# A hybrid attention and state-space layer on one core: values as plain fp32 in column halves, a strip for the S5 kernel matrix, x loaded first

## The chip, the cores and the metric

The kernel runs on one core of a Trainium2 chip. Five engines work side by side and meet through semaphores: TensorE (PE in the profile, with its weight loads as PEld), VectorE (DVE), ScalarE (ACT), GpSimd (POOL) and SyncE (SP), whose queue issues every DMA of this kernel in program order. The metric is the device time of one execution in microseconds (us), as a median over runs.

## The reference, cut to what matters

One decoder layer over 512 positions of width 1024, all in fp32:

```python
h = rmsnorm(x, norm1_g) * (1 + sc1) + sh1            # sc1, sh1 from silu(c) @ w_ada + b_ada
zq, zkc, zvc, zks, zvs, zkw, zvw, zg, zs = split(h @ w_in)
# attention: 8 query heads, 2 key/value heads, width 64, causal
#   three branches per head: compressed blocks, selected blocks, window
o_b = softmax(q k_b^T / 8, mask_b) @ v_b;   o = sum over b of gate_b * o_b
# state space: 32 groups of 16 channels, one 64-wide complex diagonal state per group
x_t = a * x_(t-1) + B u_t;   y_t = Re(C x_t) + d * u_t     # then gelu and glu
x = x + gt1 * (concat(rmsnorm(o), rmsnorm(y)) @ w_o)
h = rmsnorm(x, norm2_g) * (1 + sc2) + sh2
x = x + gt2 * ((silu(a) * b) @ w_down),  a, b = causal_conv3(h @ w_up)
return rmsnorm(x, normf_g)
```

With 512 positions all 8 blocks of 64 keys are selected and the window covers everything, so "selected" and "window" are two causal attentions with their own keys and values.

## The kernel before, in words

The work is written as named tasks, and the string `ORDER` lists them. A scheduler takes them in that order and sets each engine's own instruction stream; every engine then runs its stream strictly in order. A table `PICK` names, for single operations, the engine or the buffer pool that differs from the default. Buffers come from rings, and a load waits until the ring's next slot is free: `raw` has 4 slots of 512 KB, `unit` (weights split in two) has 4, `pt` has 4.

Most products are made of three fp32r matmuls (`mm3`, lines 120 to 123): both operands are split into a high and a low part, by a copy on ACT and a subtraction on DVE or POOL (`split`, line 109). Some products are single fp32 matmuls, each of which stands in the trace as two matmul instructions.

1. Start. Tasks `x`, `xn`: load the four 128-row tiles of x, normalise, transpose (`xT`, L458). Tasks `a`, `p`: 512 KB weight pieces for scale and shift, multiplied by silu(c) on PE (L385), turned to columns (L394). Tasks `step`, `pw`, `ri`: the powers of the state's decay, on small tiles named `gpt`, mostly on POOL (L200), and their transposes `ri` (L317). Task `bct`: transposes of B and C (`bt<-raws`, L336). Task `ws`: the state-space columns of `w_in`. Task `z`: 8 steps, each scaling one 128-row slab of xT into h (`hh`, `hl`) and making 12 matmuls of 512 columns into the four `zs` banks.
2. `W`: matrices of powers times B, made on POOL (L348, L349) and transposed on PE; `U`: u re-laid; `L`: the states within chunks of 8 positions; `chain`: the scan over the 64 chunks; `zk`, `zv`, `zq`: the other columns of `w_in`; `hid`, `comp`: the compressed keys and values.
3. Attention, 16 units (4 query tiles `qt`, 2 groups `g`, 2 pairs of heads `hp`). `S`: scores (L832), mask and maximum on DVE (L846), exponentials on ACT. `O`: for each of the qt+1 key tiles four transposes (L882) of the weights into one PSUM bank, a split of it into `pt` (L109), and four matmuls of 256 columns (L892). There the values `VT` stand as [high | low], 64 + 64 columns, so the result has the high part's product in PSUM rows 0 to 63 and the low part's in rows 64 to 127; both heads lie side by side in the columns. After each unit the low half is copied out (`tl`) and added to the high half (`oT`, L906). There are 40 key-tile steps in the 16 units.
4. State-space output, placed between the attention units: `K` makes the kernel matrices K(0) to K(7) of each group; `M` holds them as a block triangle, 8 x 8 blocks of 16 x 16 per group; `Y` multiplies u by M and the chunk states by `VV` in fp32, with the two halves of the groups in the two column halves of PE (`ps[hf * 64:(hf + 1) * 64, ...]`, L1004). M is cleared on POOL (L954); for every 4 groups, K's rows are copied out in eight small pieces `kt` (L990 and L67), d on the diagonal is added there, and eight DMAs, one per block row r, write (r+1) blocks each.
5. `gl`, `R`, `F`, `N`: glu, output projection, residual, second norm. Then up (`up`, `eup`), convolution, and down (`dn`).

## Time and profile before

| | |
|---|---|
| median of 3 runs | 789.72 us (788.53 to 789.72) |
| profiled execution, own time | 788.76 us |
| its span, first to last instruction | 787.0 us |
| busy: PE, DVE, ACT, POOL | 715.0, 503.1, 308.9, 310.7 us |
| mean granted TensorE clock | 0.949 of full speed |

The profile gives, per engine, which instructions ran, how long, and what ended the idle time before them. "L109" is line 109 of the kernel; a helper's line is shared by all that call it, so the tile names tell the tasks apart. Busy times of matmuls are modelled and overlap, so the distance between two starts says more than a matmul's own duration. The granted clock is given as a share of full speed.

### The profile page before, as it was taken

What the parts mean: (1) busy time and instruction counts of PE and PEld (TensorE: products, weight loads), DVE (VectorE), ACT (ScalarE), POOL (GpSimd) and SP (SyncE); (2) the same over time, 40 slices, a digit from 0 to 9 for tenths busy, and PEclk for the clock granted to TensorE, in tenths of its full rate; (3) what the DMA queues carried; (4) which work ended last, traced back from release to release, by engine and by line L of the source; (5) the groups of instructions that cost most, each with busy time, mean ns of one, the idle gap of its engine ahead of it and who ended that gap; (6) DMA issues with size and microseconds to landing.
All of it is one profiled execution on the core that took longest, in us unless ns stands there. A gap on an engine that the chain in (4) does not pass through costs nothing.

```text
span 787.0 us, 11037 instructions
## 1 busy us (share of the span) xinstructions
PE 715.0 (91%) x3947; PEld 582.9 (74%) x3947; DVE 503.1 (64%) x1135; ACT 308.9 (39%) x648; POOL 310.7 (39%) x318
## 2 busy tenths in 40 slices
...
GB/s 301 316 243 121 81 142 174 328 184 2 20 13 29 4 19 253 51 1 1 6 198 123 53 161 104 114 131 134 106 131 85 107 105 111 107 83 105 53 1 107
DMA packets 30458, 86.69 MB, mean 110 GB/s; under 512 B 8296, under 2 KB 8740, under 8 KB 30373
## 3 DMA queue, kind: packets, MB, share of 16 engines
...
HBM read 82.71 MB, written 2.10 MB: 108 GB/s over the span
## 4 chain that ended last, share of the span: by engine, by line
PE 66%; DVE 17%; POOL 7%; ACT 4%; issue 4%; DMA 1%; SPq 0%; POOLq 0%; DVEq 0%; ACTq 0%
PE up L123 9%; PE up L121 9%; PE up L122 9%; PE dn L122 5%; PE dn L123 5%; PE dn L121 5%; DVE Ss L846 2%; PE pv L892 1%; PE eup L123 1%; PE eup L122 1%; PE eup L121 1%; PE y L1004 1%; POOL gpt L200 1%; PE sc L832 1%; PE zs L121 1%
## 5 line engine op out<-in xcount | busy, mean ns | idle before, releaser
L121 PE MATMUL up<-h2h,uup 128*128 128x512 f32 x320 | 126.5, 395 | 0.0
L122 PE MATMUL up<-h2l,uup 128*128 128x512 f32 x320 | 126.3, 395 | 0.0
L123 PE MATMUL up<-h2h,uup 128*128 128x512 f32 x320 | 126.2, 394 | 0.0
L1167 DVE SCALAR_TENSOR_TENSOR us<-up,cst,us 128x511 f32<-128x511 f32 x80 | 59.8, 747 | 63.0 <-ACT us L1165 61.9
L1165 ACT ACTIVATE us<-up,cst 128x512 f32<-128x512 f32 x40 | 31.1, 778 | 107.3 <-PE up L123 107.2
L123 PEld LDWEIGHTS up<-h2h,uup 128*128 128x128 f32 x320 | 60.1, 188 | 14.1
L122 PEld LDWEIGHTS up<-h2l,uup 128*128 128x128 f32 x320 | 60.0, 188 | 14.1
L121 PEld LDWEIGHTS up<-h2h,uup 128*128 128x128 f32 x320 | 60.1, 188 | 14.0
L122 PE MATMUL dn<-udn,ghs 128*128 128x512 f32 x176 | 68.5, 389 | 0.0
L123 PE MATMUL dn<-udn,ghs 128*128 128x512 f32 x176 | 68.5, 389 | 0.0
L121 PE MATMUL dn<-udn,ghs 128*128 128x512 f32 x176 | 68.0, 389 | 0.0
L109 DVE TENSOR_TENSOR uup<-rup,uup 128x1024 fp32r<-128x1024 f32 x32 | 40.9, 1280 | 13.3 <-ACT uup L64 13.1
L73 POOL TENSOR_SCALAR Ss<-Ss,sm 128x384 f32<-128x384 f32 (+3 forms) x40 | 25.1, 641 | 47.3 <-DVE sm L855 34.2
L71 POOL CAST uup<-rup 128x1024 fp32r<-128x1024 f32 x6 | 7.1, 1186 | 82.6 <-PE up L123 80.4
L121 PEld LDWEIGHTS dn<-udn,ghs 128*128 128x128 f32 x176 | 33.0, 188 | 6.9
L122 PEld LDWEIGHTS dn<-udn,ghs 128*128 128x128 f32 x176 | 33.0, 188 | 6.9
L123 PEld LDWEIGHTS dn<-udn,ghs 128*128 128x128 f32 x176 | 33.0, 188 | 6.8
L832 PE MATMUL sc<-KS,QS 128*128 128x288 f32 (+2 forms) x128 | 33.2, 373 | 5.2 <-DVE mx L846 2.2
L892 PE MATMUL pv<-pt,VT 128*128 128x256 f32 x160 | 33.3, 314 | 3.0 <-DVE pt L109 1.3
L851 ACT ACTIVATE Ss<-Ss,mx 128x128 f32<-128x128 f32 (+3 forms) x64 | 35.0, 550 | 0.0
L109 DVE TENSOR_TENSOR udn<-rdn,udn 128x1024 fp32r<-128x1024 f32 x17 | 22.4, 1316 | 19.0 <-ACT udn L64 11.2
L64 ACT ACTIVATE uup<-rup 128x1024 fp32r<-128x1024 f32 x28 | 29.4, 1049 | 9.4 <-PE up L123 8.1
...
## 6 DMA issues: line engine op xcount, KB each, us to landing
rup<-in_w_up_dram SPq DMA_DIRECT2D x44, 512.0 KB, 3.3
rdn<-in_w_down_dram SPq DMA_DIRECT2D x22, 512.0 KB, 3.2
mid<-in_w_ada_dram SPq DMA_DIRECT2D x16, 512.0 KB, 4.0
adap<-in_w_ada_dram SPq DMA_DIRECT2D x8, 512.0 KB, 7.5
adaa<-in_w_ada_dram SPq DMA_DIRECT2D x8, 512.0 KB, 8.5
adag<-in_w_ada_dram SPq DMA_DIRECT2D x8, 512.0 KB
adab<-in_w_ada_dram SPq DMA_DIRECT2D x7, 512.0 KB, 3.6
xt<-in_x_dram SPq DMA_DIRECT2D x4, 512.0 KB, 5.5
```

The costliest lines, as they stand in the source:

```text
L64: A.activation(dst, src, AF.Copy, **({} if s is None else {"scale": s}))
L73: P.tensor_scalar(dst, src, s, 1.0, op0=ALU.mult, op1=ALU.mult)
L109: eng.tensor_tensor(out=lo, in0=src, in1=f(hi), op=ALU.subtract)
L121: PE.matmul(ps, w[0], m[0], start=start, stop=False)
L122: PE.matmul(ps, w[0], m[1], start=False, stop=False)
L123: PE.matmul(ps, w[1], m[0], start=False, stop=stop)
L832: PE.matmul(ps[:, :n], v.QS[:, h, qs], v.KS[:, g, x, c0:c0 + n], start=x == 0, stop=x == 1)
L846: V.tensor_tensor_reduce(out=dst, in0=src, in1=msk, scale=1.0, scalar=init, op0=ALU.add, op1=ALU.max, accum_out=ao)
L851: A.activation(Sv[:, br, :nk], Sv[:, br, :nk], AF.Exp, bias=mx[:, e, 1 + br:2 + br], scale=0.125, accum_out=sm[:, e, 1 + br:2 + br])
L892: PE.matmul(po[:, :256], VT[:, kc, br, g], pT[:, x, br * 256:(br + 1) * 256], start=kc == 0 and br == 0 and x == 0, stop=kc == qt > 0 and ...
L1165: A.activation(u_, ps, AF.Identity, bias=cv[:, 3, c_:c_ + 1], scale=cv[:, 2, c_:c_ + 1])
L1167: V.scalar_tensor_tensor(u_[:, d:], ps[:, :S - d], cv[:, 2 - d, c_:c_ + 1], u_[:, d:], op0=ALU.mult, op1=ALU.add)
```

## The change

Seven things.

- Order of the start: x is loaded first and normalised before anything else; the loads of a, p and ws follow in the order in which the z steps use them, and z steps stand between them in `ORDER`. The pieces of a and p, which before were spread over `raw` and `pt`, are nearly all in `raw` now. h's low part `hl` (8 subtractions of 128x512) is made on DVE and no longer on POOL; squares of x are summed on ACT and no longer on DVE; x is scaled on ACT and DVE, no longer on POOL.
- Attention, `O`: `VT`, `VC` and the transposed weights stay fp32 and whole. A key-tile step copies the PSUM bank once (14 of the 40 copies on DVE, 26 on ACT), and makes four fp32 matmuls of 64 x 128 columns; head e of the pair writes PSUM rows 64e to 64e+63. The four units of a query tile share one bank, which is copied out once (`oT`).
- `K` and `M`: d enters as four more small matmuls per 4 groups (`dg`), K's bank is copied whole into a strip with 112 zeros ahead of it (`kz`), and one DMA per group and half writes 64 partitions of 512 bytes, each reading the strip 16 elements further on. M is not cleared any more.
- `W`: four steps of 8 groups and two halves of 4 powers, channel ahead of power in the layout, power 0 taken as 1 from the table `RI`; the four small copies on POOL go. 24 operations of 512 elements instead of 24 of 448.
- `zu`: u is laid out with the position innermost, to match W.
- The three operations of one of the eight `VV` steps go from DVE to POOL; five subtractions of the up weights go from DVE to POOL, two of the down weights too.
- `ORDER` differs in many places behind the start as well.

```diff
@@ ORDER, first lines @@
-x3 ident c rows x0 x1 x2 sp bc step vt silu p1 dT pw ri a1 bct0 xn0 xn1 bct1 a0 p0 xn2 ws1 Bb1 ws3 xn3 ws0 z0 z1 z2 z3 a2 p2 a3 ws2 p3 z4 z5
+ident c x0 xn0 x1 xn1 x2 xn2 x3 xn3 rows sp vt silu a0 p0 ws0 step a1 p1 z0 z1 ws1 z2 dT a2 p2 z3 ws2 pw bc a3 p3 z4 z5 ws3 ri bct0 bct1 z6
...
-        v.Z2 = v.zu[:, 0].rearrange("p (g r c) -> p g r c", r=4, c=C)
+        v.Z2 = v.zu[:, 0].rearrange("p (g c r) -> p g c r", r=4, c=C)
...
-        v.scv = p2.tile([128, 2, 2, 4, T, C], F32, tag="x", name="scv")
-
-    @per("W", *range(8))
-    def _(gq):
+        v.scv = p2.tile([128, 2, 8, 2, C, 4], F32, tag="x", name="scv")
+        P.memset(RI[:, 0, 0], 1.0)
+        P.memset(RI[:, 0, 1], 0.0)
+
+    @per("W", 0, 1, 2, 3)
+    def _(q):
         v.nw = getattr(v, "nw", 0) + 1
-        wb, wt = v.scv[:, v.nw % 2, 0], v.scv[:, v.nw % 2, 1]
-        we = kn(f"e_W{gq}", "P", "V")
-        cpy(kn(f"e_Wc{gq}", "P", "A", "V"), wb[:, :, 0], Bb1[:, gq * 4:gq * 4 + 4])
-        powers(wb[:, :, 1:], Bb1, Bb2, gq * 4, 4, 1, T - 1, wt[:, :, 1:], EN[we])
-        ps = psum(f"W{gq}", f"W{gq}", "ms", "tr")
-        for g in range(4):
-            PE.transpose(ps[:, g * 128:(g + 1) * 128], wb[:, g].rearrange("p t c -> p (t c)"), ident)
-        cpy(kn(f"e_We{gq}", "A", "V"), v.W[:, gq * 4:gq * 4 + 4], ps.rearrange("p (g n) -> p g n", g=4))
+        wb = v.scv[:, v.nw % 2]
+        for h in range(2):
+            tmp = sw(f"wt{q}{h}").rearrange("p (g c t) -> p g t c", g=8, c=C)
+            powers(wb[:, :, h].rearrange("p g c t -> p g t c"), Bb1, Bb2, q * 8, 8, 4 * h, 4, tmp, EN[kn(f"e_W{q}{h}", "P", "V")])
+        for hf in range(2):
+            ps = psum(f"W{q}{hf}", f"W{q}{hf}", "ms", "tr")
+            for g in range(4):
+                PE.transpose(ps[:, g * 128:(g + 1) * 128], wb[:, hf * 4 + g].rearrange("p h c t -> p (h c t)"), ident)
+            cpy(kn(f"e_We{q}{hf}", "A", "V"), v.W[:, q * 8 + hf * 4:q * 8 + hf * 4 + 4], ps.rearrange("p (g n) -> p g n", g=4))
...
-    VT = p1.tile([128, NT, 2, 2, 128], F32R, tag="vt", name="VT")
+    VT = p1.tile([128, NT, 2, 2, 64], F32, tag="vt", name="VT")
...
-        split(VT[:, t, :, :, 0:64], VT[:, t, :, :, 64:128], src, V)
+        cpy(kn(f"e_VT{t}", "A", "V"), VT[:, t], src)
...
+    def half_pt(n, name):
+
+        if v.pT is None:
+            v.pT = pt([128, 2, 512], F32, name)
+            return v.pT[:, 0, :n]
+        p, v.pT = v.pT[:, 1, :n], None
+        return p
...
-        po = psum("pv", f"pv{un}", "pv")
-        pc_ = psum(f"pc{un}", f"pc{un}", "tr", "pv", "ms")
+        if qt not in v.po:
+            v.po[qt] = psum(f"po{qt}", f"po{qt}", "pv", "ms", "acc")
+        c = slice(u * 128, (u + 1) * 128)
+
+        def half(e):
+            return v.po[qt][e * 64:(e + 1) * 64, c]
+        pc_ = psum(f"pc{un}", f"pc{un}", "tr", "ms", "acc")
         PE.transpose(pc_[:, :128], scz[ui], ident)
-        pz = pt([128, 2, 128], F32R, f"pz{un}")
-        split(pz[:, 0], pz[:, 1], pc_[:, :128], V)
+        pz = (p2.tile([128, 256], F32, tag="ada", name=f"pz{un}", bufs=kn("b_ada", 2, 1, 3, 4)) if kn(f"pz{un}", "ada", "sw") == "ada" else sw(f"pz{un}"))[:, :128]
+        cpy(kn(f"e_pz{un}", "A", "V"), pz, pc_[:, :128])
         for kc in range(qt + 1):
-            pc_ = psum(f"p{un}{kc}", f"p{un}{kc}", "tr", "ms")
+            pc_ = psum(f"p{un}{kc}", f"p{un}{kc}", "tr", "ms", "acc")
             for br in range(2):
                 for e in range(2):
                     o = (br * 2 + e) * 128
                     PE.transpose(pc_[:, o:o + 128], v.Ss[:, ui, e, br, kc * 128:(kc + 1) * 128], ident)
-            pT = pt([128, 2, 512], F32R, f"pt{un}{kc}")
-            if kn(f"e_pt{un}{kc}", "V", "P") == "P":
-                ps_ = sw(f"ps{un}{kc}")
-                cpy(kn(f"e_ps{un}{kc}", "A", "V"), ps_, pc_)
-                split(pT[:, 0], pT[:, 1], ps_, P, kn(f"h_ps{un}{kc}", "A", "P"))
-            else:
-                split(pT[:, 0], pT[:, 1], pc_, V)
+            pT = half_pt(512, f"pt{un}{kc}")
+            cpy(kn(f"e_pT{un}{kc}", "AV"[kc % 2], "VA"[kc % 2]), pT, pc_)
             for br in range(2):
-                for x in range(2):
-                    PE.matmul(po[:, :256], VT[:, kc, br, g], pT[:, x, br * 256:(br + 1) * 256],
-                              start=kc == 0 and br == 0 and x == 0, stop=kc == qt > 0 and br == 1 and x == 1)
+                for e in range(2):
+                    o = (br * 2 + e) * 128
+                    PE.matmul(half(e), VT[:, kc, br, g], pT[:, o:o + 128], start=kc == 0 and br == 0, stop=kc == qt > 0 and br == 1)
             if kc == 0:
                 for e in range(2):
-                    for x in range(2):
-                        PE.matmul(po[:, e * 128:(e + 1) * 128], VC[:, g, e], pz[:, x], start=False,
-                                  stop=qt == 0 and e == 1 and x == 1)
-        tl = (p2.tile([128, 256], F32, tag="ada", name=f"tl{un}", bufs=kn("b_ada", 2, 1, 3, 4)) if kn(f"tl{un}", "ada", "sw") == "ada" else sw(f"tl{un}"))[:64, :256]
-        cpy(kn(f"e_tl{un}", "A", "V"), tl, po[64:128, :256])
-        eo, hi_ = V, po[0:64, :256]
-        if kn(f"e_oT{un}", "V", "P") == "P":
-            eo, hi_ = P, sw(f"th{un}")[:64, :256]
-            cpy(kn(f"e_th{un}", "A", "V"), hi_, po[0:64, :256])
-        for e in range(2):
-            eo.tensor_tensor(out=oT[e * 64:(e + 1) * 64, 2 * g + hp], in0=hi_[:, e * 128:(e + 1) * 128],
-                             in1=tl[:, e * 128:(e + 1) * 128], op=ALU.add)
+                    PE.matmul(half(e), VC[:, g, e], pz, start=False, stop=qt == 0)
+        v.no[qt] = v.no.get(qt, 0) + 1
+        if v.no[qt] == 4:
+            v.oT[qt] = p1.tile([128, 4, 128], F32, tag="oT", name=f"oT{qt}", bufs=kn("b_oT", 3, 4, 2))
+            cpy(kn(f"e_oT{qt}", "A", "V"), v.oT[qt].rearrange("p c n -> p (c n)"), v.po[qt])
...
     @task("M")
         v.M = p2.tile([128, G, T, C], F32, tag="h0", name="M")
-        P.memset(v.M, 0.0)
...
-        for n, (o, w) in enumerate(((0, C), (C, 112))):
+        for n, o, w in ((1, C, 112), (0, 0, C)):
             for g in range(4):
                 g_ = gq * 4 + g
                 m = v.VV[:, g_, 0:T - 1].rearrange("p t c -> p (t c)") if n else C1[:, g_]
-                PE.matmul(ps[32 * g:32 * g + 32, o:o + w], Bb1[:, g_:g_ + 2].rearrange("p g c -> p (g c)"), m, start=True, stop=True,
+                PE.matmul(ps[32 * g:32 * g + 32, o:o + w], Bb1[:, g_:g_ + 2].rearrange("p g c -> p (g c)"), m, start=True, stop=n == 1,
                           tile_position=(0, 32 * g))
-        kt = p1.tile([16, 4, T, C], F32, tag="sw", name=f"kt{gq}", bufs=kn("b_sw", 3, 4, 5))
+        dg = p1.tile([16, 4, C], F32, tag="dg", name=f"dg{gq}", bufs=2)
+        EN[kn(f"e_dg{gq}", "V", "P")].tensor_tensor(out=dg, in0=bc(ident[:16, 0:1], (0, 4), (1, C)), in1=bc(dT[:, gq * 4:gq * 4 + 1], (1, 4), (0, C)), op=ALU.mult)
         for g in range(4):
-            row = ps[32 * g:32 * g + C]
-            V.scalar_tensor_tensor(kt[:, g, 0], ident[:C, 0:C], dT[:, gq * 4 + g:gq * 4 + g + 1], row[:, 0:C], op0=ALU.mult, op1=ALU.add)
-            cpy("AV"[g % 2], kt[:, g, 1:].rearrange("p t c -> p (t c)"), row[:, C:128])
-        for r in range(T):
-            nc.sync.dma_start(v.M[r * C:(r + 1) * C, gs, T - 1 - r:], kt[:, :, 0:r + 1])
+            PE.matmul(ps[32 * g:32 * g + 32, 0:C], ident[0:C, 0:32], dg[:, g], start=False, stop=True, tile_position=(0, 32 * g))
+
+        if gq % 2 == 0 or v.kz is None:
+            v.kz = sw(f"kz{gq}")[:, :480].rearrange("p (a n) -> p a n", a=2)
+            EN[kn(f"e_kz{gq}", "P", "V")].memset(v.kz[:, :, 0:112], 0.0)
+            v.nk = 0
+        kz = v.kz[:, v.nk]
+        v.nk += 1
+        if v.nk == 2:
+            v.kz = None
+        cpy(kn(f"e_kt{gq}", "A", "V"), kz[:, 112:240], ps[:, :128])
+        for g in range(4):
+            for hf in range(2):
+                o = kz[32 * g:32 * g + C, hf * 64:hf * 64 + 1]
+                nc.sync.dma_start(v.M[hf * 64:hf * 64 + 64, gq * 4 + g].rearrange("p t c -> p (t c)"), bc(o, (C, 4), (1, 128)))
```

SP's stream at the start, before; `adap` and `adaa` are pieces of p and a, `rins` of ws, `raws` holds B and C:

```order
L168 DMA xt<-in_x_dram 128x1024 x3
L204 DMA sp<-in_ssm_dram 32x145
L208 DMA raws<-in_bc_dram 32x4096
L370 DMA adap_150<-in_w_ada_dram 128x1024
L370 DMA adap_152<-in_w_ada_dram 128x1024
L370 DMA adaa_222<-in_w_ada_dram 128x1024
L370 DMA adaa_224<-in_w_ada_dram 128x1024
L370 DMA adaa_319<-in_w_ada_dram 128x1024
L370 DMA adaa_321<-in_w_ada_dram 128x1024
L115 DMA rins_374<-in_w_in_dram 128x1024
```

And the same place now:

```order
L168 DMA xt<-in_x_dram 128x1024 x4
L164 DMA rows<-in_vec_dram 108x128
L204 DMA sp<-in_ssm_dram 32x145
L370 DMA adaa_201<-in_w_ada_dram 128x1024
L370 DMA adaa_203<-in_w_ada_dram 128x1024
L370 DMA adap_220<-in_w_ada_dram 128x1024
L370 DMA adap_222<-in_w_ada_dram 128x1024
L208 DMA raws<-in_bc_dram 32x4096
L596 DMA cst<-in_cst_dram 128x768
L370 DMA adac_769<-in_w_ada_dram 128x1024
L115 DMA rins_238<-in_w_in_dram 128x1024
L370 DMA adaa_263<-in_w_ada_dram 128x1024
```

The first ws piece stands behind one a and one p now, and the four `raw` slots are full when it comes.

PE's stream at the start, before, from the first a and p products on:

```order
L385 MATMUL mp_154<-adap_150,cs 32x256 x4
L385 MATMUL mp_154<-adap_152,cs 32x256 x4
L385 MATMUL ma_226<-adaa_222,cs 32x256 x4
L458 MATMUL xT_268<-ident,xt 128x128 x4
L394 MATMUL mp_154<-ones,rowp_155 128x1 x2
L385 MATMUL ma_226<-adaa_224,cs 32x256 x4
L458 MATMUL xT_274<-ident,xt 128x128 x4
L317 MATMUL ri<-ident,gpt 128x32
L336 MATMUL bt_241<-ident,raws 128x32 x16
```

And now, from the last transposes of x to the first z product; a further `ri`, the second `bt` and a1's columns stand between these two pieces:

```order
L458 MATMUL xT_181<-ident,xt 128x128 x4
L317 MATMUL ri<-ident,gpt 128x32
L336 MATMUL bt_538<-ident,raws 128x32 x16
L254 MATMUL vt<-ident,rows 128x108
L385 MATMUL ma_205<-adaa_201,cs 32x256 x4
L385 MATMUL ma_205<-adaa_203,cs 32x256 x4
L385 MATMUL mp_224<-adap_220,cs 32x256 x4
L385 MATMUL mp_224<-adap_222,cs 32x256 x4
```

```order
L385 MATMUL ma_267<-adaa_263,cs 32x256 x4
L385 MATMUL ma_267<-adaa_265,cs 32x256 x4
L385 MATMUL mp_286<-adap_282,cs 32x256 x4
L394 MATMUL ma_267<-ones,rowa_268 128x1 x2
L121 MATMUL zs_300<-uins_240,hh 128x512
```

All transposes of x now precede the a and p products, and the first a product stands behind `ri` and `bt`.

DVE's stream in the third query tile's units, before: each `pt` row is the second half of a split, the copy on ACT being the first:

```order
L846 ISA Ss,mp_3472<-sc_3479,cst,mp_3472 128x256
L846 ISA mp_3472 128x1
L109 TENSOR_TENSOR pt_3155<-p_3150,pt_3155 128x512
L846 ISA Ss,mp_3472<-sc_3479,cst,mp_3472 128x256
L846 ISA mp_3472 128x1
L846 ISA Ss,mx_3470<-sc_3484,cst,mp_3472 128x128
L846 ISA mx_3470 128x1
L109 TENSOR_TENSOR pt_3167<-p_3162,pt_3167 128x512
```

And now, in another unit of that query tile, where `pt` on DVE is a copy and stands alone:

```order
L67 COPY pt_2950<-p_2945 128x512
L848 ISA Ss,mx_3046<-sc_3055,cst,mp_3048 128x256
L848 ISA mx_3046 128x1
L848 ISA Ss,mx_3046<-sc_3071,cst,mp_3064 128x256
L848 ISA mx_3046 128x1
L848 ISA Ss,mx_3046<-sc_3055,cst,mp_3048 128x256
L848 ISA mx_3046 128x1
L67 COPY pt_2950<-p_2956 128x512
```

One `pt` buffer now takes two steps' weights, where before it took the high and the low part of one.

## Rows read from the trace of the kernel before

**Rows 1.** Busy by stage: length, PE, PEld, DVE, ACT, POOL, clock, DMA share, GB/s.

```profile
0.00:43.70 43.70, 25.60 (x200) 16.20 (x200) 21.15 (x55) 22.47 (x43) 31.22 (x61) 1.00 0.88 312
43.70:72.00 28.30, 27.59 (x136) 25.83 (x133) 20.81 (x24) 7.64 (x13) 28.14 (x31) 0.94 0.52 171
72.00:120.00 48.00, 48.00 (x338) 40.59 (x337) 24.90 (x42) 21.33 (x45) 35.41 (x38) 1.00 0.38 116
120.00:185.00 65.00, 53.42 (x388) 36.91 (x386) 43.72 (x59) 11.83 (x26) 51.07 (x55) 0.87 0.60 202
185.00:240.00 55.00, 40.23 (x282) 31.39 (x283) 48.56 (x238) 33.24 (x121) 23.14 (x19) 0.77 0.08 14
240.00:400.00 160.00, 145.52 (x924) 121.43 (x924) 134.76 (x457) 98.25 (x250) 77.08 (x76) 0.94 0.16 53
400.00:770.00 370.00, 369.60 (x1669) 306.78 (x1669) 198.00 (x245) 108.55 (x141) 60.09 (x36) 0.99 0.31 104
```

**Rows 2.** PE in order of time, 0 to 100 us: start, length, instruction.

```profile
14.57 2.27 PE L385 MATMUL mp<-adap,cs 128*32 128x256 f32 x16 [3.14 <-DMA adap<-in_w_ada_dram]
...
21.87 0.31 PE L317 MATMUL ri<-ident,gpt 32*128 32x32 f32 x1
22.00 1.93 PE L336 MATMUL bt<-ident,raws 32*128 32x32 f32 x16
...
43.69 0.63 PE L121 MATMUL zs<-uins,hh 128*128 128x512 f32 x1
...
71.81 0.39 PE L123 MATMUL zs<-uins,hl 128*128 128x512 f32 x1
72.03 1.04 PE L544 MATMUL W<-ident,scv 128*128 128x128 f32 x8
```

**Rows 3.** DMA issues by line: size, median us from issue to landing.

```profile
rup<-in_w_up_dram SPq DMA_DIRECT2D x44, 512.0 KB, 3.3
```

**Rows 4.** POOL in order of time, around 20 us.

```profile
20.21 0.58 POOL L200 TENSOR_TENSOR gpt<-gpt,sp 32x64 f32<-32x64 f32 x2
```

**Rows 5.** POOL, groups by form, 30 to 180 us: count, busy us, mean ns.

```profile
L348 POOL TENSOR_TENSOR scv<-RI,Bb 128x448 f32<-128x448 f32 x14 | 15.5, 1115 | 0.1
L109 POOL TENSOR_TENSOR hl<-scr,hh 128x512 fp32r<-128x512 f32 x8 | 10.4, 1310 | 0.0
...
L71 POOL COPY zu<-X 64x1024 f32<-64x1024 f32 x2 | 4.9, 2436 | 0.1
```

**Rows 6.** DVE, groups by form, 180 to 400 us.

```profile
L109 DVE TENSOR_TENSOR pt<-p,pt 128x512 fp32r<-128x512 f32 x37 | 24.8, 680 | 1.4 <-ACT pt L64 1.3
...
L990 DVE SCALAR_TENSOR_TENSOR kt<-ident,dT,K 16x16 f32<-16x16 f32 x32 | 7.1, 223 | 2.0 <-PE K L985 0.7 <-ACT kt L64 0.6
...
L906 DVE TENSOR_TENSOR oT<-pv,tl 64x128 f32<-64x128 f32 x20 | 5.6, 278 | 0.2
...
L109 DVE TENSOR_TENSOR pz<-pc,pz 128x128 fp32r<-128x128 f32 x16 | 4.5, 280 | 0.5 <-ACT pz L64 0.4
...
L67 DVE COPY kt<-K 16x112 f32<-16x112 f32 x16 | 4.2, 264 | 0.0
...
L67 DVE COPY tl<-pv 64x256 f32<-64x256 f32 x9 | 3.8, 424 | 2.3 <-PE pv L892 1.9 <-issue 0.3
...
L67 DVE COPY Y<-y 128x512 f32<-128x512 f32 x2 | 1.4, 678 | 0.0
```

**Rows 7.** PE in order of time, 240 to 262 us.

```profile
245.21 0.56 PE L897 MATMUL pv<-pz,VC 128*128 128x128 f32 x4
245.60 0.68 PE L892 MATMUL pv<-pt,VT 128*128 128x256 f32 x4
246.12 0.60 PE L882 MATMUL p<-ident,Ss 128*128 128x128 f32 x4
246.65 0.44 PE L1004 MATMUL y<-M,zu 128*64 128x128 f32 x4
...
248.55 0.33 PE L874 MATMUL pc<-ident,scz 128*128 128x128 f32 x1
```

More of the change, by code (lines that the diff above doesn't have):

```diff
@@ L426, in _ @@
     def _():
-        v.gt1 = p2.tile([128, 2, D], F32, tag="x", name="gt1")
+        v.gt1 = p2.tile([128, 1, D], F32, tag="x", name="gt1")
         for hf in range(2):
@@ L702, in _ @@
             madd(Xb[:, k, 1:], k, (cy[:, 0, 0:1], 32), 7, f"a{k}", EN[kn(f"e_a{k}", "PV"[k % 2], "VP"[k % 2])])
-    VC = p1.tile([128, 2, 2, 128], F32R, tag="vc", name="VC")
+    VC = p1.tile([128, 2, 2, 64], F32, tag="vc", name="VC")
     @task("VC")
     def _():
-        EN[kn("e_VC", "V", "P")].memset(f(VC), 0.0)
+        EN[kn("e_VC", "V", "P")].memset(VC, 0.0)
     @task("cw")
@@ L773, in _ @@
             src = po[rows, :128].rearrange("p (g n) -> p g n", g=2)
-            A.activation(VC[rows, :, e, 0:64], src, AF.Copy, scale=0.5)
-            V.scalar_tensor_tensor(VC[rows, :, e, 64:128], src, 0.5, f(VC)[rows, :, e, 0:64], op0=ALU.mult, op1=ALU.subtract)
+            cpy(kn(f"e_VC{e}", "A", "V"), VC[rows, :, e], src, 0.5)
     @per("zq", 0, 1, 2, 3)
```

43 lines of the change are left out of this document (21 added, 22 removed).

## The prediction

> **What bounds the kernel now.** I read the busy times by stage first. From 400 to 770 us PE is busy 369.6 of 370 us at a clock of 0.99, and the change adds or removes no PE work there [rows 1]. So nothing is to be had behind 400 us, and whatever is won has to be won ahead of it and then stays won. Ahead of 400 us the stages differ. To 43.7 us the DMA engines are at 88% with 312 GB/s and PE is busy 25.6 us: PE waits for loads and for the small chain that feeds it. From 72 to 120 us PE is busy without a gap. From 120 to 185 us it is busy 53.4 of 65 us. From 185 to 240 us DVE is busy 48.6 of 55 us (88%) and PE 40.2 us at a clock of 0.77: DVE sets the pace. From 240 to 400 us DVE has 84% and PE 91% at 0.94: both are near their limit [rows 1].
>
> Second, the stream of PE in order of time: the first z product starts at 43.69 us and the last ends where W's transposes begin, at 72.03 us [rows 2]. Third, the groups on DVE in the attention stages, which say what the change takes from it [rows 6].
>
> The sum is made against the profiled execution's own time, 788.76 us (a span of 787.0 and 1.76 outside it), which is 0.96 us below the median of 789.72.
>
> **The start.** All work of z is 96 matmuls at 0.22 to 0.24 us (71.81 to 72.03 is one [rows 2]), 23 us in all. The question is when they can start, and whether a, p and ws keep up. In the new PE stream the first a product stands behind `ri` and `bt`. `ri` needs the first power, which POOL finishes at 20.21 + 0.58 = 20.8 us [rows 4]; the steps ahead of it change engine but not number, so I leave that time. Then `bt` takes 1.93 us, to 22.7, and a quarter of a0 and p0 takes 2.27/4 = 0.57 us [rows 2]. At 23.3 us the first `raw` slot is free and ws0 can be issued; 3.3 us later it lands [rows 3], at 26.6. Three more pieces (a1, a1, p1) come behind it, at 524 KB over 312 GB/s = 1.7 us each [rows 1], to 31.7, and their products stand ahead of z0 on PE; so z0 starts at about 32 to 33 us. From there PE has 23 us of z, and two and a quarter more sets of a and p; a set (two a and two p pieces) is 32 instructions, 4.5 us at the pace of 14.57 us [rows 2], half of it at a full clock, so 5 to 10 us. The sum is 60 to 66; I take 63 us for the end of z, 9 us ahead of 72. The bounds: 57 if everything but z hides, 72 if the ring of four slots with a, p and ws in it feeds PE no faster than before. So the term is -9, from 0 to -15. PE is full from there to 120 us [rows 1], which keeps it.
>
> POOL must keep up too, since W's transposes wait for it. It loses the 8 `hl` subtractions, 10.4 us, and its 3 scalings of x; W's operations grow from 448 to 512 elements, a seventh of 15.5 us and of as long again for the rest of that group, 3 to 4 us [rows 5]. That is 6 us less, so the L products are not held up. What the trace does not show is a two-input operation on POOL that writes or reads at 16-byte steps, as W's will, with the power innermost in memory and the channel innermost in the loop. The nearest row is the copy with a strided read, 2436/1024 = 2.4 ns per element, against 1115/448 = 2.5 ns for W's products [rows 5]. The lower bound is therefore 1.27 us for 512 elements, the upper the two added, 2.5 us; I take 1.4, by the row that it is nearest to. The Trainium skill (GPSIMD Engine Reference, section "Performance pitfalls for Q7 kernels") says that a kernel on that engine which reads at steps above 8 bytes pays about half as much again per element; by it the 7 additions of W on POOL alone would grow by some 0.6 us each, an estimate of 4 us, still inside the 6 that go. The row of the strided copy neither confirms nor excludes it.
>
> **O: what goes from DVE.** 37 subtractions `pt` at 680 ns, 24.8 us; 16 `pz`, 4.5 us; 28 additions `oT` (20 in the row, 8 of the same form in the last query tile), 28 x 278 ns = 7.8 us; 9 copies `tl`, 3.8 us. From K: 32 + 16 instructions on `kt`, 7.1 + 4.2 = 11.3 us. With one VV step moved to POOL, 2 us, that is 54 us [rows 6]. What comes: 14 copies of a PSUM bank at the 678 ns of `Y<-y`, 9.5 us; 6 copies of K and 2 of `pz` at 280 ns, 2.2 us; one `oT`, 0.7; `dg`, moved scalings and an addition, about 3. So 15 us come, and 39 us of DVE's 183 us from 185 to 400 us go [rows 1]. ACT loses 11 copies net and the small K copies; POOL loses the clearing of M and gains a few, and has room at 47% [rows 1].
>
> **O and K on PE.** The y products have the new form, fp32 with 64 columns in either half. Between 246.65 and 248.55 us there are eight rows of four instructions, 16 products, so 0.119 us each [rows 7]: the two halves run side by side. Four of them per key-tile step take 0.48 us, where four fp32r products took 246.12 - 245.60 = 0.52; with VC, two for four (0.39 us from 245.21), 40 steps and 16 units give 40 x 0.04 + 16 x 0.15 = 4 us less. Against that, PE changes form: four transposes from 246.12 to 246.65 take 0.53 us where their own spacing would be about 0.4, and from the last y to the transposes at 248.55 it looks no longer than 0.1. I take 0.11 us per change of form, both ways; the new order has 70 changes at the PV products and 22 more around y, 92 x 0.11 = 10 us. The 32 small `dg` products I put at 2 us. PE gets 8 us more, at worst 92 x 0.2 = 18. The Trainium skill (TensorEngine Tiling (Array Packing), section "Key Properties") states that changing the tiling mode drains TensorE; the trace agrees, with the 0.1 us of that gap, and the page gives no price; without a drain the sum would be 10 us lower on PE, and the last rival would not stand.
>
> **Sum for the attention.** Where DVE sets the pace (185 to 240 us) the 39 us come off almost one for one: all of K is there and the first five or six units' splits, some 18 us off and 5 back, so -12 of 55. From 240 to 400 us 26 us net come off DVE, but PE is busy 145.5 of 160 us and gets most of the 8 us; a third of the saving, -8, with +3 from PE's own work, is -5. Together -17, a little under half of what DVE loses. The bounds are -4 (PE's order and the latency of each unit hold the pace) and -28 (three quarters of DVE's loss).
>
> **The rest, at nothing.** M's DMAs go from 64 in growing strips to 64 of 32 KB; y follows the transposes directly and waits for no load [rows 7], and SP has nothing else to issue there. If that cover goes, one landing, 3.3 us [rows 3], shows once. The clearing of M leaves POOL, which is 42% busy then. The up and down subtractions moved to POOL lie under a full PE, with POOL at 16% [rows 1].
>
> Sum: 788.76 - 9 - 17 = 762.8; I say 763 us.
>
> **Rivals.**
> The ring holds the start: a, p and ws share four slots, and z ends at 72 as before. For it: the first slot is freed only at 23.3 us, and the loads ahead of ws0 (x, a0, p0, B and C, the constants, one more piece: 5.8 MB) are through at 312 GB/s by 19 us, so DMA then stands still. Against: the loads are used in the order in which they come. Time: 788.76 - 17 = 772.
> The attention is not DVE's: each unit's chain from scores to exponentials to transposes sets the pace, with two score buffers as before, and DVE's relief gives only 4. For it: PE's clock of 0.77 and its gaps go with chains, not one engine. Against: DVE at 88%. Time: 788.76 - 9 - 4 = 776.
> POOL's strides: W's 21 operations on POOL at 2.5 us are 52 us where they would be 25 at 1.2, 27 more; less the 10 of `hl`, W ends 17 us later than before, and PE, in order, stands before W's transposes. With half of that filled by the products that stand ahead of them, -9 turns into +8. For it: no row shows such an operation. Against: the strided copy's row. Time: 788.76 + 8 - 17 = 780.
> Slower: the change of form. If 92 changes cost 0.35 us each (a transposed tile's own 0.33 us to pass through, as at 248.55 [rows 7]), PE gets 32 + 2 - 4 = 30 us more, becomes the only bound from 185 us on, and DVE's relief buys nothing: 788.76 - 9 + 30 = 810. With DVE's relief gone it turns slower from (9 + 4 - 2)/92 = 0.12 us a change on, which is near the 0.11 that I take; what speaks against it is that PE stands idle for a quarter of 185 to 240 us and runs at 0.77 there, so that DVE's relief cannot be worth nothing.
>
> **How the numbers follow.** My forecast 0.62; the ring 0.12; the unit's chain 0.15; POOL's strides 0.05; the change of form 0.06. The range reaches from 746 (-15 and -28) to 778 (the first two rivals); the rest lies mostly above. About 0.2%, 1.6 us, is what a measurement of this kernel can tell from no change: faster 0.92, same 0.02, slower 0.06.
>
> **What would show it.** The first z product near 33 us and the first zk product near 63; W's last transposes not waited for by PE, and L's products 9 us earlier; the first `pt` copies with no DVE partner; DVE's busy time down by about 35 us with the same work behind 400; the stretch from the last z to the first `eup` product shorter by 17. I would be wrong if PE's wait ahead of z has a new name (a load of p, or the first power), or if PE's busy time between 185 and 400 us rises by more than 10.

## The result: a third of the forecast gain

The changed kernel takes 781.21 us (781.01 to 781.52, 4 runs) against 789.72 (788.53 to 790.68): a ratio of 0.9893, 95% interval 0.9876 to 0.991. It is faster by 8.5 us where I had forecast 26.7, and lies above my range. The profiled execution has a span of 779.3 us, 7.7 below the 787.0 of before.

First its busy time by stage (length, PE, PEld, DVE, ACT, POOL with instruction counts, granted clock, DMA share, GB/s). I cut at the first z, the last z, the last L, the last hid, the last zq and the first eup product:

```profile
0.00:35.90 35.90, 22.02 (x137) 15.38 (x138) 11.86 (x40) 22.45 (x38) 16.07 (x48) 1.00 0.78 246
35.90:78.70 42.80, 37.39 (x211) 30.89 (x211) 31.87 (x37) 18.29 (x34) 35.80 (x36) 0.96 0.64 227
78.70:118.40 39.70, 39.01 (x252) 32.37 (x253) 25.88 (x36) 12.92 (x26) 27.11 (x27) 1.00 0.34 118
118.40:158.20 39.80, 34.75 (x302) 24.01 (x304) 25.17 (x35) 11.04 (x27) 34.94 (x46) 1.00 0.65 223
158.20:199.40 41.20, 32.76 (x163) 24.38 (x166) 32.73 (x37) 7.65 (x12) 35.21 (x24) 0.83 0.33 123
199.40:391.80 192.40, 172.38 (x1423) 131.87 (x1423) 143.10 (x570) 113.78 (x329) 79.94 (x85) 0.97 0.17 52
391.80:779.30 387.50, 375.51 (x1696) 311.44 (x1696) 206.11 (x260) 112.46 (x153) 86.43 (x50) 0.98 0.30 104
```

The kernel before, cut at the same events where it differs most (z, and zq to eup):

```profile
43.70:72.20 28.50, 27.79 (x138) 25.99 (x135) 20.81 (x24) 7.77 (x13) 28.27 (x32) 0.94 0.52 170
194.80:398.20 203.40, 175.76 (x1168) 145.05 (x1169) 173.86 (x675) 128.33 (x364) 91.00 (x93) 0.90 0.14 43
```

z starts 7.8 us earlier than before [rows 2] but takes 42.8 us instead of 28.5, and ends 6.5 us later. From there PE is full to L's end, as before [rows 1], so the delay is handed on: L ends at 118.4 instead of 111.0, and zq at 199.4 instead of 194.8, +4.6 us. The stage from zq to eup is 11.0 us shorter, and what follows 1.3 (388.8 to 387.5). The sum, +4.6 - 11.0 - 1.3, is the -7.7 of the spans. So the start, forecast at -9, is a loss, and the attention gives two thirds of its -17.

What holds z shows on DVE, in order of time (start, length, engine, line, instruction):

```profile
36.42 0.16 DVE L400 TENSOR_TENSOR mod<-mod,vt 128x2 f32<-128x2 f32 x1
...
60.95 2.08 DVE L109 TENSOR_TENSOR uins<-rins,uins 128x1024 fp32r<-128x1024 f32 x1
62.95 0.15 DVE L399 TENSOR_TENSOR mod<-ma,bsc 128x2 f32<-128x2 f32 x1
63.02 3.10 DVE L109 TENSOR_TENSOR uink<-rink,uink 128x1024 fp32r<-128x1024 f32 x1
66.04 2.05 DVE L400 TENSOR_TENSOR mod<-mod,vt 128x2 f32<-128x2 f32 x1
68.02 0.15 DVE L403 TENSOR_TENSOR mod<-mp,vt 128x2 f32<-128x2 f32 x1
68.09 1.21 DVE L109 TENSOR_TENSOR uink<-rink,uink 128x1024 fp32r<-128x1024 f32 x1
```

on POOL at the time of the later ones:

```profile
61.91 6.18 POOL L349 TENSOR_TENSOR scv<-scv,wt 128x512 f32<-128x512 f32 x2
```

and on PE (the brackets give the idle time ahead and its releaser):

```profile
65.19 0.60 PE L547 MATMUL W<-ident,scv 128*128 128x128 f32 x4
68.22 0.66 PE L547 MATMUL W<-ident,scv 128*128 128x128 f32 x4 [2.43 <-DVE mod L403]
70.30 0.81 PE L121 MATMUL zs<-uins,hh 128*128 128x512 f32 x1 [1.42 <-ACT hh L64]
70.91 0.63 PE L122 MATMUL zs<-uins,hh 128*128 128x512 f32 x1
71.33 0.63 PE L121 MATMUL zs<-uins,hh 128*128 128x512 f32 x1
```

Read them together. The last scale and shift for z (`mod`) stand on DVE behind the subtraction of a weight that zk needs only at 79 us. An operation on 256 numbers, L400, takes 2.05 us: it ends when POOL's second addition ends, at 68.09. L399 and L403, of the same size, take 0.15; each has one operand in PSUM, L400 has both in SBUF. The same L400 took 0.16 us at 36.42, when POOL stood idle. So while POOL adds, DVE's operations with two SBUF inputs wait for it, one after the other. The Trainium skill (SBUF — State Buffer, section "SBUF: two separate sides") says that a DVE operation with two SBUF inputs and a POOL operation that reads SBUF exclude each other for the whole instruction; these rows agree (2.05 us against 0.16). PE then stands 2.43 and 1.42 us, and the eight products behind it start 0.43 us apart instead of 0.235, at the lower of the clock's two levels (granted 0.50 from 70.3 to 73.5 us). POOL's addition ends 0.08 us ahead of `mod` and could be what PE waits for first; run e6 below speaks against it, as these transposes start there at 65.97, 0.06 us behind `mod`, and POOL's addition goes on to 67.81.

W's steps on POOL by form (count, busy, mean ns), to set against [rows 5]:

```profile
L349 POOL TENSOR_TENSOR scv<-scv,wt 128x512 f32<-128x512 f32 x7 | 17.4, 2516 | 0.1
L348 POOL TENSOR_TENSOR wt<-RI,Bb 128x512 f32<-128x512 f32 x7 | 9.5, 1385 | 1.1 <-DVE scv L349 1.0
L348 POOL TENSOR_TENSOR scv<-RI,Bb 128x512 f32<-128x512 f32 x7 | 8.8, 1281 | 0.0
```

The products write at 16-byte steps and cost what they cost before: 1.10 us each in the quiet pair at 84.45 us, against 0.99 for 448 elements at 75.42 before, which would be 1.13 for 512. The additions also read at 16-byte steps: 2.52 us, and 2.1 where they lose no time to DVE. A pair of them, and a pair from run e5 below, where the addition alone goes in the order of memory (there it stands in line 350):

```profile
86.59 4.26 POOL L349 TENSOR_TENSOR scv<-scv,wt 128x512 f32<-128x512 f32 x2
82.91 2.48 POOL L350 TENSOR_TENSOR scv<-scv,wt 128x512 f32<-128x512 f32 x2
```

2.13 us against 1.24 is 72% more. The Trainium skill's rule on steps (GPSIMD Engine Reference, "Performance pitfalls for Q7 kernels") says half as much again; these rows show the cost, and show it larger.

In the attention, PE in order of time:

```profile
258.01 0.53 PE L834 MATMUL sc<-KS,QS 128*128 128x288 f32 x2
258.47 0.66 PE L901 MATMUL po<-pt,VT 128*64 128x128 f32 x8
258.96 0.39 PE L904 MATMUL po<-pz,VC 128*64 128x128 f32 x4
259.28 0.73 PE L834 MATMUL sc<-KS,QS 128*128 128x512 f32 x2
```

Eight instructions are four products, 0.49 us from 258.47 to 258.96, 0.12 each as read from [rows 7]. The form changes cost little too: the four instructions after it take 0.32 us up to 259.28 where 0.24 is theirs, 0.08 for the change.

### The profile page after: what moved, and what is told of

Read it like the earlier page. It is cut to its first block, busy times and chain, and to the rows that moved or that the text cites. A ratio compares the mean times of both kernels' runs of the same rounds, so it can differ in the third digit from the quotient of the medians.

```text
span 779.3 us, 11258 instructions
## 1 busy us (share of the span) xinstructions
PE 713.8 (92%) x4171; PEld 570.3 (73%) x4171; DVE 476.7 (61%) x1011; ACT 298.6 (38%) x617; POOL 315.5 (40%) x312
## 4 chain that ended last, share of the span: by engine, by line
PE 72%; DVE 9%; POOL 6%; DMA 6%; ACT 4%; issue 3%; SPq 0%; POOLq 0%; ACTq 0%; DVEq 0%
PE up L123 10%; PE up L121 10%; PE up L122 9%; PE dn L123 5%; PE dn L122 5%; PE dn L121 5%; PE po L901 2%; PE sc L834 2%; PE p L895 2%; DMA raws<-in_bc_dram 2%; POOL prl L689 1%; PE eup L121 1%; PE y L1015 1%; PE eup L122 1%; PE eup L123 1%
## 5 line engine op out<-in xcount | busy, mean ns | idle before, releaser
L109 POOL TENSOR_TENSOR uup<-rup,uup 128x1024 fp32r<-128x1024 f32 x13 | 32.8, 2525 | 64.7 <-ACT uup L64 51.4
L109 DVE TENSOR_TENSOR uup<-rup,uup 128x1024 fp32r<-128x1024 f32 x27 | 37.1, 1375 | 14.8 <-ACT uup L64 14.7
L73 POOL TENSOR_SCALAR Ss<-Ss,sm 128x384 f32<-128x384 f32 (+3 forms) x38 | 23.2, 622 | 42.0 <-DVE sm L857 24.7
L109 POOL TENSOR_TENSOR udn<-rdn,udn 128x1024 fp32r<-128x1024 f32 x7 | 17.2, 2458 | 54.7 <-DVE udn L67 27.2
L109 DVE TENSOR_TENSOR udn<-rdn,udn 128x1024 fp32r<-128x1024 f32 x15 | 19.9, 1328 | 17.1 <-ACT udn L64 10.4
```

The source lines that it names most:

```text
L73: P.tensor_scalar(dst, src, s, 1.0, op0=ALU.mult, op1=ALU.mult)
L109: eng.tensor_tensor(out=lo, in0=src, in1=f(hi), op=ALU.subtract)
```

## The experiments

Theories of the start: D, DVE's queue and POOL's hold on it; R, the ring of four slots; W, POOL's steps and through them L; P or Z, PE's fixed order, so that an earlier W buys nothing. The scheduler works out the whole order anew for each kernel, so a part tried alone is also tried in another order; where an order strays far from the changed kernel's, the text says so.

**The parts undone and alone.**

```diff
 e1: the changed kernel, ORDER up to W and PICK of x, a, p, z as before
 e2: the kernel before, with that ORDER and PICK as changed
 e3: the kernel before
-    split(pT[:, 0], pT[:, 1], pc_, V)   (and V, VC, oT)
+    cpy(..., pT, pc_)                    the value products alone
 e4: the kernel before
-    kt strips and P.memset(v.M, 0.0)
+    kz = sw(...); cpy(..., kz[:, 112:240], ps[:, :128])
```

In e4 the rows of M stand in another order than U's, so its y is not the reference's; the work is the same.

> The changed kernel with the start of the kernel before: its order of tasks up to W and its choice of engines and buffers for x, a, p and z; everything from W on as changed. Theory S: the new start itself loses time (z ends 6.5 us later, zq 4.6 us later than before, because the last two pairs of z wait on VectorE and on loads), so with the old start zq ends 4 to 6 us earlier than in the changed kernel and the time is 775 to 778 us. Rival W: the start is good for 8 us and W's new layout (strided additions on GpSimd) eats it; then the old start makes it worse, 783 to 790 us, and the end of zq moves later than 199.4. Rival N: a later zq is absorbed by the attention's own limit; then 780 to 782 us whatever zq does.

> The kernel before with the new start alone (W in its old layout, old attention, old K). Theory S: zq ends 4 to 6 us later than in the kernel before and the time is 793 to 796 us. Rival W: the new start alone is a gain, 780 to 784 us. Rival N: 789 to 791 us.

> The kernel before with the fp32 value products alone (V and VC not split, a head in each half, one copy per transposed tile); K and M, W and the start as before. By my prediction's sizes O takes about 30 of the 39 us off VectorE, so if VectorE is what bounds 185 to 240 us it gives 8 to 13 us: 777 to 782 us. Rival: K and M give most of the gain (they take 11 us off VectorE ahead of the first y); then O alone gives under 4 us, 786 to 790 us. Rival: change of form on TensorE costs what VectorE gives; then 789 us or more.

> The kernel before with the new K and M alone (one copy of K's bank into a zero-led strip, 64 loads of 32 KB, no clearing of M); O as before. The dg tile lies in a free part of RI, one buffer instead of two. If K and M are a small part, 0 to 3 us: 787 to 790 us. Rival: they give most of the gain, 780 to 784 us, with y ending 6 us or more earlier.

Measured: e1 789.14 us (ratio 1.0001, 0.9981 to 1.0021), e2 801.11 (1.0137, 1.0118 to 1.0156), e3 782.91 (0.992, 0.9896 to 0.9944), e4 789.11 (1.0003, 0.9982 to 1.0025). O alone gives 6.6 us, less than the 8 to 13 that I expected; K and M give nothing by themselves. The start taken alone costs 11.6 us, yet putting the old start back costs 8: theory S, which expected 775 to 778 us of e1, is wrong in that direction. e1 falls into rival W's range, with zq later as it said (203.4); e2 falls into none. In e1 z ends at 75.8, but L only at 122.7 (118.4 in the changed kernel). POOL has both the eight `hl` and W's dearer steps there, and W on POOL ends at 102.4; PE's waits between z and L are 3.2 us for a copy of `zu` on DVE and 1.1 for W. In e2 z ends at 73.4 and L at 108.3, ahead of the kernel before (111.0); what e2 loses comes behind L (zq at 202.3, eup at 412.1), in an order that is neither kernel's, so its 11.6 us are no price of the start.

The two runs do divide the stretch of z. It takes 28.5 us before, 30.0 with the new W alone, 37.0 with the new start alone, and 42.8 with both. The stretch in e1, then in e2 (columns as above):

```profile
45.70:75.70 30.00, 28.25 (x138) 25.92 (x135) 20.99 (x20) 7.38 (x11) 28.57 (x23) 0.94 0.43 145
36.40:73.40 37.00, 34.42 (x203) 29.43 (x203) 18.05 (x28) 17.89 (x34) 31.22 (x45) 0.95 0.72 249
```

In e2 the eight `hl` are on DVE as well, yet DVE is busy 18.05 of 37.0 us and PE waits in that stretch for a load (1.3 us) and for ACT (1.3), not for DVE. So `hl` on DVE does not hold z by itself; it does together with W's dearer steps. The parts don't add up to the whole.

**Mending the start, one thing at a time.**

```diff
 e5: W's addition in the order of memory
-    eng.tensor_tensor(out=dst, in0=dst, in1=tmp, op=ALU.add)
+    a, b = nat or (dst, tmp)
+    eng.tensor_tensor(out=a, in0=a, in1=b, op=ALU.add)
 e6: no chain of two operations for a scale
-    V.tensor_tensor(mod, ps, bsc, add); V.tensor_tensor(mod, mod, vcol, mult)
+    V.tensor_scalar(mod[:, 0, j:j + 1], ps[:, e:e + 1], bsc[...], vcol(norm, 1, j), op0=ALU.add, op1=ALU.mult)
 e8: +'r_adaa00': 'pt', 'r_adap00': 'pt', ... (10 of 16 pieces)
 e9: all three
```

> The changed kernel, with the third operation of each W step (the addition of the two products) run in the order of memory instead of at 16-byte steps; the products still write at 16-byte steps, and nothing is left out. The changed kernel's additions took 2.52 us each on GpSimd (7) and 2.77 on VectorE (1). Theory W (the steps of the addition hold W, and W holds the L products): each addition falls to 1.3 to 1.5 us, W's last transposes end 6 to 8 us earlier than 112.3, L ends near 111 instead of 118.4, and the time is 774 to 777 us. Rival P (the additions fall, but TensorE's own order, full from 79 to 120 us, sets the end of zq): W earlier, zq within 1.5 us of 199.4, 780 to 782 us. Rival: the step makes no difference to GpSimd: additions stay above 2 us.

> The changed kernel, with each scale of the first norm worked out by one operation per column (add, then multiply, in one instruction) in place of two chained ones, so that VectorE's queue has no weight subtraction between the two. Theory D (VectorE's in-order queue holds the last pair of z): the last pair of z starts 2 us earlier than 70.3, z ends near 76.5, and if TensorE is full behind it zq ends 2 us earlier and the time is 779 us. Rival P: z ends earlier but the end of zq stays within 1 us, 781 us.

> The changed kernel, with 10 of the 16 loaded pieces for a and p in the second ring of buffers (as in the kernel before), so that a, p and ws no longer share four slots; the scheduler's order on TensorE moves with it. Theory R (the ring paces z, one pair per 9 to 12 us where its products take 7.6 at most): pairs of z follow at under 9 us and z ends by 70 instead of 78.7. If z's end is what matters the time falls to 773 to 777 us; if W's (L ends 118.4 as before), it stays at 780 to 783 us.

> The three edits together: additions in the order of memory, one operation per scale, ten pieces in the second ring. If the start's loss is made of the three and each counts, zq ends near 188 to 192 and the time is 769 to 773 us, below both kernels. If only one of them binds, it equals the best of the single ones within 1.5 us. If the scheduler's new order gives it back, 778 us or more.

Measured: e5 802.12 (1.0162, 1.0141 to 1.0182), e6 783.05 (0.9927, 0.9905 to 0.9949), e8 800.31 (1.0134, 1.0116 to 1.0151), e9 785.09 (0.9936, 0.9913 to 0.9958). No mend beats the changed kernel. The additions in e5 did fall, to 1.24 us where DVE is quiet, and W on POOL ended at 90.0 instead of 97.1; but the scheduler, which now counts on that, put K's first products between zq's on PE, and there the waits of e5 say (waiter, releaser, total, times, longest):

```profile
PE K L988 <- DVE VV L350: 11.0, 1, 11.0
```

zq ended at 220.1. In e6, whose PE order differs in a few rows only, z ended 2.4 us earlier as theory D said, but W's transposes then waited 1.7 us for POOL's addition and L ended at 119.2: z's tail and W bind within 2 us of each other. e8 speaks against the ring: the loads came faster (318 and 306 GB/s in the first two 20-us slices, 267 and 235 before the edit), the first z at 35.6 us was no earlier, and z ended at 82.8; but the scheduler also turned the powers later (44.9 us for 40.1), and PE's mean clock over z was 0.86 where it was 0.96, so this is no clean test of R. e9 shows the same early loads, z's end at 76.0 and zq at 199.1, as in the changed kernel; its profiled execution is the fastest of its six (780.80 us, median 785.09). e8 lost behind z as well: its stage from zq to eup took 210 us instead of 192, with PE at a lower mean clock on nearly the same work:

```profile
202.90:265.60 62.70, 54.79 (x569) 41.98 (x569) 47.20 (x237) 33.89 (x130) 20.74 (x29) 0.76 0.19 35
```

against this in the changed kernel:

```profile
199.40:254.00 54.60, 49.48 (x586) 37.42 (x586) 41.59 (x239) 35.81 (x140) 14.25 (x24) 0.94 0.21 41
```

e2 shows the same 210 us, at a mean clock of 0.89. What in these two orders makes it was not tried, and stays open.

**The same order, less on DVE.** Taking W's one step on DVE back to POOL together with e5's edit leaves PE's and DVE's order as it was but for a few rows: the clean test.

```diff
 e10, e15: e5's edit, and
-    'e_W11': 'V'
 e11: the same, and e6's edit
 e12: the same as e11, and
+    'e_hl6': 'P'
 a0: the changed kernel again, beside e15
```

> The changed kernel with all of W's steps on GpSimd (one of eight stood on VectorE, 6.8 us of it between 47 and 59 us) and W's additions in the order of memory; nothing left out. The order on TensorE and VectorE stays that of the changed kernel but for a few rows, so what moves here is not the scheduler's order. Theory D (VectorE, busy 11.97 of 12 us from 58 to 70, holds the last pair of z, and z's end holds all that follows to zq): the last pair starts 2 to 5 us earlier than 70.3, z ends at 74 to 77 instead of 78.7, zq ends at 195 to 198 and the time is 777 to 780 us. Theory W (GpSimd's W holds L): W on GpSimd ends near 95 (97.1 before), its additions at 1.3 us, gain 2 us at most. Rival P (TensorE's order): no change in zq within 1 us, 781 us.

> The same with one operation per scale of the first norm (in the changed kernel a weight's subtraction of 3.1 us stands between the two chained ones). Theory D: another 1 to 2 us off z's end, which is then 72 to 75; zq ends at 194 to 197, 776 to 779 us. Rival: z's end moves and zq does not: 780 to 782 us.

> The same with one of the eight lower-half subtractions of z (the seventh, 1.1 us on VectorE in the changed kernel) back on GpSimd as in the kernel before. Theory D: VectorE's full stretch is 1 us shorter; 775 to 779 us. If GpSimd is the limit by then, W ends 1.3 us later and the time is 778 to 781 us.

> The changed kernel itself, once more, as the base for the three beside it on the same chip: 781 to 783 us.

> The kernel with all of W's steps on GpSimd and its additions in the order of memory, once more. If relieving VectorE between 47 and 70 us is worth what the profile showed (z ends 3.9 us and zq 2.8 us earlier), its median lies 1.5 to 3 us below that of the changed kernel beside it; if that was one execution's luck, within 1 us.

Measured: e10 779.81 (0.9877, 0.9857 to 0.9897), e11 782.93 (0.992, 0.9892 to 0.9948), e12 782.81 (0.9917, 0.9895 to 0.9939), a0 782.69 (0.9901, 0.988 to 0.9923), e15 779.93 (0.988, 0.986 to 0.99). The busy times of e10 in the stretch where DVE was full (columns as above):

```profile
58.00:70.00 12.00, 9.65 (x48) 8.96 (x47) 10.84 (x12) 6.70 (x9) 11.80 (x13) 1.00 0.77 277
```

the same of the changed kernel:

```profile
58.00:70.00 12.00, 8.26 (x40) 7.62 (x40) 11.97 (x11) 6.17 (x10) 11.03 (x8) 1.00 0.65 239
```

and PE at the last pair of z, in e10 and then in e15, which is the same kernel:

```profile
65.71 0.66 PE L550 MATMUL W<-ident,scv 128*128 128x128 f32 x4 [0.93 <-DVE mod L404]
67.78 0.62 PE L121 MATMUL zs<-uins,hh 128*128 128x512 f32 x1 [1.42 <-ACT hh L64]
68.24 0.40 PE L122 MATMUL zs<-uins,hh 128*128 128x512 f32 x1
```

```profile
65.49 0.66 PE L550 MATMUL W<-ident,scv 128*128 128x128 f32 x4 [0.99 <-DVE mod L404]
67.56 0.82 PE L121 MATMUL zs<-uins,hh 128*128 128x512 f32 x1 [1.42 <-ACT hh L64]
68.18 0.63 PE L122 MATMUL zs<-uins,hh 128*128 128x512 f32 x1
```

In that stretch DVE is busy 1.1 us less and PE 1.4 us more. In e10 the chained `mod` takes 1.22 us instead of 2.05, the last pair of z starts at 67.78 instead of 70.30 and keeps the full clock, z ends 3.9 us earlier (74.8) and zq 2.8 (196.6), and the span is 2.4 us shorter. Beside a0 on one chip, e15 has z 3.6 us earlier, zq 1.3, the span 3.5 and the median 2.8, though the two intervals overlap. In e15 the last pair runs at the lower clock again, in e10 it does not, after nearly the same waits: from its first product to z's end it takes 8.3 us and 7.0, so 1.3 of e10's 3.9 us is the clock.

So theory D holds as to place, the last pair of z. What reaches the end is 1.4 us against the changed kernel's first measurement and 2.8 beside a0, near what separates the runs. The edit also ends W on POOL at 91.8 instead of 97.1, and e6, where z ended 2.4 us earlier and W on POOL did not, gained nothing; so the gain is not shown to be DVE's alone. e10 and e15 are the fastest version I have, some 10 us below the kernel before. e11 and e12 miss. e11's profile is of the slowest of its six executions (787.93 us, median 782.93). PE is at the lower clock there in three stretches more (from 43, 51 and 72 us), and z ends at 79.8; DVE is busy only 5.7 us of those 12, but 10.6 from 68 to 80, as the same work comes later. Why e11's median is no better than the changed kernel's is not shown. In e12 the moved subtraction stands on POOL behind A4 and W, and PE waits for it:

```profile
74.72 2.09 PE L123 MATMUL zs<-uins,hl 128*128 128x512 f32 x4 [5.40 <-POOL hl L109]
```

**POOL's late start.** In the changed kernel POOL stands 10.75 us, to 41.1, for the turned powers, because PE has their last four transposes behind z's first eight products. Both kernels are e10 with one edit.

```diff
 e13: +'e_pw4': 'V'
 e14: ORDER
-    U0 U1 cst A4 X W3 KS ... wv0 W2 L2 ... chain
+    U0 U1 cst X W3 W2 KS ... wv0 L2 ... A4 chain
```

> The same with the last doubling of the powers on VectorE, so that the powers are turned ahead of z's first products on TensorE. The scheduler moves later rows too (the transposes of W stand earlier on TensorE). Theory G (GpSimd's late start holds W and W holds L): Bb on GpSimd starts at 31 to 34 us instead of 40, W on GpSimd ends near 84 to 87, L ends at 105 to 110 instead of 116, and zq 4 to 8 us earlier: 772 to 776 us. Rival Z (TensorE is full from z's end on, so only z's end counts): L earlier but zq within 2 us of 196.6; 778 to 782 us. If the scheduler's other order costs more than that: 785 us or more.

> The kernel with all of W on GpSimd, and A4 (16 us of small steps between W's pieces) behind W in the order of tasks. Theory G: W on GpSimd ends near 80, L ends at 106 to 111, zq 3 to 7 us earlier: 773 to 777 us. Rival Z: L earlier, zq within 2 us of 196.6: 778 to 782 us. If the scheduler's other order costs more: 785 us or more, as in the two runs at 800.

Measured: e13 804.48 (1.0184, 1.0164 to 1.0204), e14 793.51 (1.0051, 1.0031 to 1.007). W on POOL ends early in both (89.7 and 84.7 us), and L at 112.7 in e14, where theory G puts it at 106 to 111. But e13 has the 11-us wait of K of e5 again, and zq ends at 225.4; in e14 zq waits 5.3 us for `KS` and ends at 212.7. Whether G would pay in an order kept as it was could not be tried, as every such edit moves the order.

## Why the prediction was wrong, point by point

**The start, -9: wrong in sign.** z started at 35.9 us, 2.9 after my 33, and from there took 42.8 us, where I had 30: 23 of z, about 7 of a and p (5 to 10), and nothing else. The rows give PE 37.39 us of work in those 42.8: the products of z at 0.235 us are 22.6, sixteen of them at 0.43 add 3.1 (eight at 36 us, eight at 70), W's sixteen transposes 2.3, a, p and the rest 9.4. PE stands the other 5.4, of which 3.9 are the two waits at 68 and 70 us. So the term for z's stretch left out the slower products, W's transposes and every wait, and had a and p too small. More than half of the excess comes with the new start itself: e2, which has no wait for DVE there, takes 37.0 us.

The rest, 5.8 us, comes with W, and here the step that failed is "POOL must keep up too. It loses the 8 `hl` subtractions". It asked only whether W would end in time on POOL, and it did, within 2.4 us. I took `hl` off POOL and never put it on DVE, nor W's step there, beside the weights' subtractions, and did not ask what POOL's longer additions do to DVE. From 35 to 80 us `hl` takes 7.4 us of DVE and W's step 5.9 (1.1 + 2.0 + 2.8), where the weights' subtractions take 10.4 (three of `uins`, three of `uink`); these times include waits for POOL. DVE is busy 31.87 us of z's 42.8, in e2 18.05 of 37.0. The rows show POOL's additions holding DVE ahead of z's last pair; how the 5.8 us divide between them and DVE's added work is not shown.

**POOL's strides, 1.4 us taken (1.27 to 2.5).** The products were right, 1.28 to 1.39. The additions were 2.52, at the upper end, which I did not keep apart: they read at steps, the products only write at them. W on POOL ended 2.4 us later than before (97.1 against 94.7) and not 17, as POOL had lost `hl`. The rival that I gave 0.05 names the operation that grew, but not what it did: from z's end to L's end PE waits for POOL not at all (0.5 us in a0), and the cost came through DVE. Its 780 us comes close by luck.

**The ring (0.12).** z ended later than its 72. In e8 and e9 the loads came earlier and the first z did not; the waits of the changed kernel ahead of z's last pair are `mod` and `hh`, not loads.

**The attention, -17: right in kind, too large.** DVE lost 30.8 us from zq to eup (173.86 to 143.10), against 39. The step that failed is that this relief comes off the time, "almost one for one" to 240 us and by a third behind it. Four products at 0.48 us and 0.11 us for a change of form were read rightly (0.49 and 0.08), so the slower rival is out. But the sum was never held against PE's own time. A stage of 203.4 - 17 = 186.4 us with 175.76 + 8 us of PE work leaves PE 2.6 us idle, where it had 27.6; nothing in the profile spoke for that. What came instead: PE's busy time fell by 3.4 us with the clock at 0.97 instead of 0.90, and its idle time from 27.6 to 20.0. Of the 11.0 us 7.6 are idle time and 3.4 busy time, and e3 shows 5.9 of it from O alone, with the old start and W. In e4 DVE is busy 168.13 us there, 5.7 less than before, and the stage is 1.1 us longer (204.5): K's share of the relief bought nothing. The rival that each unit's chain sets the pace (4 us, 0.15) was too small by 7 us where I was too large by 6; which waits make PE's 20.0 us of idle time was not tested.

**M, the DMAs, up and down at nothing: right.** e4 is within 0.25% of before, and from eup to the end the kernel gained 1.3 us. That e4 gains nothing fits this point, and speaks against the one above, which counted K's 11 us on DVE as a gain.

**What I listed as signs** read true on DVE's relief in the attention and on the new name of PE's wait ahead of z's last pair. I named a load or the first power for it; it was `mod`. The others missed: the first zk product came at 79.4 us and not near 63, L ended 7.4 us later and not 9 earlier, and from the last z to the first `eup` product the kernel gained 12.9 us (326.0 to 313.1), not 17.

## What to carry to other kernels

When an operation leaves one engine, write it into the sum of the engine that gets it, in that stage, with the length it has while its neighbour is busy: here a subtraction on DVE took 3.10 us beside POOL's additions and 1.21 without. Hold a forecast for a stage against the busy time of its fullest engine, and distrust it where it leaves that engine far less idle time than the profile shows (2.6 us here, where it was 27.6). Where a scheduler orders the whole kernel, a part tried alone is tried in another order; choose edits that leave the order as it was, or the order's 11 to 22 us (e5, e8, e13, e14) hide a part's 3.

## What the runs showed of the chip

DVE's operation on 256 numbers, both inputs in SBUF, took 2.05 us beside POOL's additions and 0.16 with POOL idle; with one operand in PSUM it took 0.15 beside them. A subtraction of 128x1024 took 3.10 us there and 1.21 right after POOL's addition had ended. The wait can span several of POOL's operations. One DVE addition at the same place in two executions of the changed kernel, first in its profile and then in a0's:

```profile
88.55 9.39 DVE L616 TENSOR_TENSOR ko<-rope 128x768 f32<-128x768 f32 x1
89.33 1.03 DVE L616 TENSOR_TENSOR ko<-rope 128x768 f32<-128x768 f32 x1
```

In the first, POOL ran W's products and additions one behind the other until 97.13, and DVE's addition ended at 97.94. POOL's additions that read at 16-byte steps took 2.1 us, or 2.5 to 3.1 beside DVE, and 1.24 in the order of memory; its products that only write at such steps took 1.1, as contiguous ones did. Pauses of PE of 0.93 and 1.42 us were followed by eight products at the full clock in e10, and pauses of 0.99 and 1.42 us by products at the lower clock (granted 0.50 from 67.3 us) in e15, which is the same kernel; so these runs do not say which pause brings the lower clock.
